# Neighbourhood attention in a hybrid encoder: the raw biases of a pair of heads are asked for ahead of the pair's stack transfers

## The chip, the cores and the metric

The kernel runs on one core of a Trainium2 chip. The metric is the device time of one execution in microseconds (us). The engines are called PE (TensorE), DVE (VectorE), ACT (ScalarE), POOL (GpSimd) and SP (SyncE, which here only issues DMA transfers).

## The reference

Two layers of an encoder, 512 tokens of width 1024, all in float32. Each layer has a half-step feed-forward block, a mixer of three attention branches, and a second half-step feed-forward block. The change touches branch A, the neighbourhood attention: eight heads of 64 channels, tokens laid out as 8 rows of 64 columns, each query attending to all 8 rows and to 16 columns around its own, with a bias per head that depends on the distance in rows and columns.

```python
scores = jnp.einsum('bhrcd,bhrijd->bhrcij', qg, kg).astype(jnp.float32) * (d ** -0.5)
bias = rpb[:, dr[:, None, :, None], dc[None, :, None, :]]
scores = scores + bias[None].astype(jnp.float32)
scores = jnp.where(col_ok[None, None, None, :, None, :], scores, NEG)
p = jax.nn.softmax(scores.reshape(b, h, rows, GRID_W, kr * GRID_W), axis=-1)
out = jnp.einsum('bhrcij,bhrijd->bhrcd', p, vg)
```

## The kernel before

A float32 product is made of three fp32r matmuls (L322, L323, L324), each operand split into a high and a low half. These, called dense matmuls below, fill PE; the attention's own small matmuls are woven between them. The mixer is a list of units in a string, ORDER, that begins "qa0 qa1 aa0 aa1 qa3 qa2 aa3 aa2"; `do(u)` builds one unit after the other. Unit qa*i* makes the projections of head pair *i* (in `qkv_a`), unit aa*i* its attention (`attn_a`, which calls `softmax_pv` once for each of its two heads). Inside the mixer a scheduler sets the order on each engine from the dependences and its own costs, so the order of the text is only one of its inputs.

- `stacks(x, both)` splits a projection into hi (ACT, L348) and lo (DVE, L349) and copies the halves with DMAs on SP's queue into stacked tiles st and sw (L1342, L1343, L1347, L1348). A pair needs four for the queries and eight for the keys, 128 KB each.
- `turn` transposes the values (L1355) and splits them (ACT L1361, DVE L1362).
- `softmax_pv` computes four blocks of scores (L1385, two matmuls each). DVE adds the bias and keeps the extremum nmx (L1388), ACT takes the exponential (L1397), DVE scales by the reciprocal (L1402, L1404), PE transposes (L1412), the halves hi and lo of the transposed block are made (L348, L349) and PE multiplies the values with them (L1415 with hi, L1416 with lo).
- `biases(hd)` loads braw, the raw bias of one head, 256 KB, on SP's queue (L1450), and makes from it and two mask tiles the tiles bedge and bmid with four DVE operations (L1458).

The masks, braw, bedge and bmid all come from one pool with tag "g" of ten buffers, so a late request for a buffer waits until an early user of it is done. The scores' PSUM banks (tag "at") are three, so the third and fourth score block wait for DVE to read an earlier one.

Of the kernel before, what the change touches and what calls it, by code (L numbers as in the profile page):

```python
# [62 lines left out]
RPBW = 64  # L63
# [52 lines left out]
def encoder_kernel(ctx: ExitStack, tc: tile.TileContext, order, xT, wts, cols, rows, rpb, consts, tables, out):  # L116
    nc = tc.nc
# [25 lines left out]
    def nm(s):  # L143
        serial[0] += 1
        return f"{s}{serial[0]}"

    def big(tag, dt=F32, shape=(P, T), name="v"):
        if tag in BUFS:
            return sb.tile(list(shape), dt, tag=tag, name=nm(name), bufs=BUFS[tag])
        kind, pool = phase[0]  # L150
        return pool.tile(list(shape), dt, tag=tag, name=nm(name), bufs=ABUFS[kind][tag])
# [105 lines left out]
    for l in range(L):  # L257
        for which in (1, 2):
            name = f"ffn{which}_w_down"
            places = {(k, u): quarter(k, u) for k in ("11", "12", "21", "22") for u in range(KS // 2)}  # L260
            places.update({(f"n{n + 1}", u): (2 * u, HB * n) for n in range(2) for u in range(KP // 2)})
            for key, (r, c) in places.items():
                src = wts[(NSTREAM + len(extra)) // WB].rearrange("p (a b) -> p a b", a=2)
# [77 lines left out]
    def dense1(name, l, c, X, r0=0, tag="mm", midway=None):  # L341
        return dense([(name, l, r0, c)], X, (tag,), midway=midway)[0]
# [97 lines left out]
    class Handover:  # L440
# [94 lines left out]
        def turn(self, tb):  # L535

            src = self.value if self.following else self.hold
            for n in range(2):
                for k in range(HB):
                    PE.transpose(self.banks[tb][n][:, k * P : (k + 1) * P], src(tb, n)[:, k * P : (k + 1) * P], ident)  # L540
# [893 lines left out]
    def mixer(l, op, first):  # L1434
# [7 lines left out]
        for c0, n in ((0, 512), (512, 256)):  # L1442
            m = big("g", name="mask")
            nc.sync.dma_start(m[:, :n], tables[:, 1024 + c0 : 1024 + c0 + n])
            for b in range(0, n, 256):
                masks[(c0 + b) // 256] = m[:, b : b + 256]

        def biases(hd):
            raw = big("g", name="braw")
            nc.sync.dma_start(raw, bass.AP(rpb.tensor, (l * 8 + hd) * 16 * RPBW, [[RPBW, 8], [1, 16], [1, 8 * RPBW]]))  # L1450
            edge = big("g", name="bedge")
            mid = big("g", shape=(P, 2 * P), name="bmid")

            def put(dst, mask, n0, n1):

                src = raw[:, 7 * RPBW + 39 - 8 * n0 :]
                (ps0, pn), _ = src.ap
                V.tensor_tensor(  # L1458
                    out=dst.rearrange("p (d r c) -> p d r c", r=8, c=8),
                    in0=bass.AP(src.tensor, src.offset, [[ps0, pn], [-8, n1 - n0], [-RPBW, 8], [-1, 8]]),  # L1460
                    in1=mask.rearrange("p (d r c) -> p d r c", r=8, c=8),
                    op=ALU.add,
                )

            put(edge[:, 0:256], masks[0], 0, 4)
            put(mid, masks[1], 0, 4)
            put(edge[:, 256:384], masks[2][:, :P], 2, 4)
            put(edge[:, 384:512], masks[2][:, P:], 0, 2)
            return lambda i: edge[:, 0:256] if i == 0 else edge[:, 256:512] if i == NT - 1 else mid


        def plain(acc, p, scale=1.0):
            x = big("tx", name="x")
            A.activation(natural(x) if p else x, perm(acc) if p else acc, AF.Copy, scale=scale)
            return x
# [12 lines left out]
        def qkv_a(q, k, v):  # L1488
            sq, sk = stacks(plain(q, True, 0.125), False), stacks(rolled(k), True)
            return sq, sk, turn(rolled(v), 2)  # L1490
# [3 lines left out]
        def attn_a(p, sq, sk, vof):  # L1494
            o = big("t", name="o")
            for s in range(2):
                softmax_pv(
                    sq[s], sk[s], lambda j, s=s: vof(j, s), biases(2 * p + s), 1.0, None,
                    perm(o[64 * s : 64 * s + 64, :]), natural, SEEN_A,
                )  # L1500
            OT["a", p] = tuple(t[:, p, :] for t in oa)
            A.activation(OT["a", p][0], o, AF.Copy)
            V.tensor_tensor(out=OT["a", p][1], in0=o, in1=f(OT["a", p][0]), op=ALU.subtract)
# [4 lines left out]
        def attn_b(p, sq, skb, vofb):  # L1508
            o = big("t", name="o")
            for s in range(2):  # L1510
                hd = 2 * p + s
                kv = hd // 4
                softmax_pv(
                    sq[s], skb[kv], lambda j, kv=kv: vofb(j, kv), bias_b, 0.125,
                    (sink[:, l, hd : hd + 1], nsink[:, l, hd : hd + 1]),
                    o[64 * s : 64 * s + 64, :], lambda ap: ap, SEEN_B,
                )
            OT["b", p] = split(o, "g")
# [58 lines left out]
        def gates(n, *ms):  # L1577
            for m in ms:
                pg = dense1(w, l, GL + n * KD + m, X)
                t = gate0[m // 4][:, m % 4, :] if n == 0 else big("g", name="gate")  # L1580
                A.activation(t, pg, AF.Tanh, scale=0.5, bias=col("b_gate", l, n * KD + m))
                gate[n, m] = t

        def combine(n, key, *ms):
            for m in ms:
                py = dense1("w_branch", l, m, [OT[key, k] for k in range(4)], r0=n * 4)
                t = gate.pop((n, m))
                V.scalar_tensor_tensor(out=t, in0=t, scalar=1.0, in1=py, op0=ALU.add, op1=ALU.mult)
                if n == 0:
                    merged[m] = t  # L1590
                else:
                    G.tensor_tensor(out=merged[m], in0=merged[m], in1=t, op=ALU.add)

        def qkv_b(c):
            return stacks(rope(dense1(w, l, c, X), cosR, sinR), c == KB)

        def qkv_c(hd):
            sq = stacks(rope(dense1(w, l, QC + hd, X), cosR, sinR), False)
            sk = stacks(rope(dense1(w, l, KC + hd, X), cosR, sinR), True)
            return sq, sk, turn(plain(dense1(w, l, VC + hd, X), False), 1)  # L1600

        def finish_c(hd):
            A.activation(totc[hd], totc[hd], AF.Sqrt)
            V.reciprocal(out=totc[hd], in_=totc[hd])
            rep = spread(totc[hd], NT)
            V.scalar_tensor_tensor(
                out=oc[hd], in0=oc[hd], scalar=gsub[:, l : l + 1], in1=rep, op0=ALU.mult, op1=ALU.mult
            )
            OT["c", hd] = split(oc[hd], "g")
# [3 lines left out]
        def do(u):  # L1613
            kind, i = u[:2], int(u[2:] or 0)
            if kind == "qa":
                if i == 0:
                    held[u] = qkv_a(*first)
                else:
                    early = second if i == 1 else []
                    late = [dense1(w, l, c + i, X) for c in (QA, KA, VA)[len(early) :]]  # L1620
                    held[u] = qkv_a(*early, *late)
            elif kind == "kb":
                held["kb"] = qkv_b(KB), turn(plain(dense1(w, l, VB, X), False), 2)
            elif kind == "qb":
                held[u] = qkv_b(QB + i)
            elif kind == "qc":
                held[u] = qkv_c(i)
            elif kind == "aa":
                attn_a(i, *held.pop(f"qa{i}"))
            elif kind == "ab":  # L1630
                attn_b(i, held.pop(f"qb{i}"), *held["kb"])
            elif kind == "ac":
                attn_c(*held.pop(f"qc{i}"))
            elif kind == "fc":
                finish_c(i)
            elif kind[0] == "g":
                gates("abc".index(kind[1]), i)
            elif kind[0] == "y":
                combine("abc".index(kind[1]), kind[1], i)

        for u in ORDER.split():
            do(u)
# [75 lines left out]
    for l in range(L):  # L1718
        with open_phase("f"):
            X, accs = ffn(l, 1, X, accs)  # L1720
        with open_phase("m"):
            X, accs = mixer(l, X, accs)
        with open_phase("f"):
            X, accs = ffn(l, 2, X, accs)
# [59 lines left out]
```

## Time and profile before

| what | us |
|---|---|
| median of 3 timed runs (2399.48 to 2400.63) | 2400.39 |
| the profiled execution | 2402.65 |
| its span from the first to the last instruction | 2400.9 |
| PE busy in it | 2373.5 |
| DVE, ACT busy | 1780.8, 1342.4 |

A busy time is a sum over instructions; the end of a matmul is modelled, so an idle time on PE shows where it waited and what a wait cost only nearly. The granted clock is 0.998 of full speed over the span. The part of layer 0 that matters lies from 355 to 430 us, that of layer 1 from 1553 to 1620 us.

### The profile page before, as it was taken

What the parts mean: (1) busy time and instruction counts of PE and PEld (TensorE: products, weight loads), DVE (VectorE), ACT (ScalarE), POOL (GpSimd) and SP (SyncE); (2) the same over time, 40 slices, a digit from 0 to 9 for tenths busy, and PEclk for the clock granted to TensorE, in tenths of its full rate; (3) what the DMA queues carried; (4) which work ended last, traced back from release to release, by engine and by line L of the source; (5) the groups of instructions that cost most, each with busy time, mean ns of one, the idle gap of its engine ahead of it and who ended that gap; (6) DMA issues with size and microseconds to landing.
All of it is one profiled execution on the core that took longest, in us unless ns stands there. A gap on an engine that the chain in (4) does not pass through costs nothing. (4 is left out here: it accounts for less than half of the span.)

```text
span 2400.9 us, 37750 instructions
## 1 busy us (share of the span) xinstructions
PE 2373.5 (99%) x14266; PEld 2080.6 (87%) x14266; DVE 1780.8 (74%) x2960; ACT 1342.4 (56%) x2493; POOL 192.7 (8%) x192
## 2 busy tenths in 40 slices
PE   9999999999999999999999999999999999999998
PEld 8999887888877889998899998878877778899987
DVE  7887975757667467888878878766676764788796
ACT  6565655646555365555655555566555554556563
POOL 0111000000111100110001110000011111011100
PEclk9999999999999999999999999999999999999999
DMA  5566536435443334664525565374354333246642
GB/s 168 161 171 187 165 139 176 128 106 154 109 133 97 100 112 140 160 167 166 171 93 167 159 176 192 118 188 118 111 146 127 107 99 123 97 144 173 186 146 90
DMA packets 119190, 340.46 MB, mean 142 GB/s; under 512 B 15968, under 2 KB 22752, under 8 KB 118496
## 3 DMA queue, kind: packets, MB, share of 16 engines
q1 hardware_dynamic: 91344, 224.72, 30.1%
q10 hardware_dynamic: 22032, 79.78, 11.0%
q0 software_dynamic: 5632, 33.56, 6.9%
q8 instruction: 112, 1.84, 0.3%
q14 instruction: 70, 0.57, 0.1%
HBM read 285.03 MB, written 48.23 MB: 139 GB/s over the span
## 5 line engine op out<-in xcount | busy, mean ns | idle before, releaser
L322 PE MATMUL mm<-X,w 128*128 128x512 f32 (+1 forms) x1044 | 396.5, 380 | 3.9 <-ACT X L618 2.1
L323 PE MATMUL mm<-X,w 128*128 128x512 f32 (+1 forms) x1044 | 396.6, 380 | 0.7 <-DVE X L550 0.7
L324 PE MATMUL mm<-X,w 128*128 128x512 f32 (+1 forms) x1044 | 396.3, 380 | 0.0
L221 DVE TENSOR_TENSOR w<-wr,w 128x512 fp32r<-128x512 f32 x360 | 255.2, 714 | 167.4 <-ACT w L220 166.1
L220 ACT ACTIVATE w<-wr 128x512 fp32r<-128x512 f32 x360 | 223.4, 627 | 224.5 <-PE mm L324 177.6
L878 PE MATMUL mm<-ht,l 128*128 128x256 f32 x1120 | 311.0, 278 | 0.0
L878 PE MATMUL mm<-ht,h 128*128 128x256 f32 x1120 | 310.9, 278 | 0.0
L878 PE MATMUL mm<-lt,h 128*128 128x256 f32 x1120 | 310.5, 277 | 0.0
L322 PEld LDWEIGHTS mm<-X,w 128*128 128x128 f32 x1044 | 197.3, 189 | 35.9 <-ACT X L549 2.6
L323 PEld LDWEIGHTS mm<-X,w 128*128 128x128 f32 x1044 | 197.3, 189 | 32.5 <-DVE X L550 1.1
L324 PEld LDWEIGHTS mm<-X,w 128*128 128x128 f32 x1044 | 197.1, 189 | 30.8
L878 PEld LDWEIGHTS mm<-lt,h 128*128 128x128 f32 x1120 | 210.7, 188 | 0.0
L878 PEld LDWEIGHTS mm<-ht,l 128*128 128x128 f32 x1120 | 210.6, 188 | 0.0
L878 PEld LDWEIGHTS mm<-ht,h 128*128 128x128 f32 x1120 | 210.5, 188 | 0.0
L1119 PE MATMUL mm<-wh,f 128*128 128x512 f32 x640 | 200.2, 391 | 0.0
L878 PE MATMUL mm<-X,h 128*128 128x256 f32 x1120 | 198.8, 277 | 0.0
L878 PEld LDWEIGHTS mm<-X,h 128*128 128x128 f32 x1120 | 169.8, 188 | 0.5 <-DVE v L932 0.2
L878 PE MATMUL mm<-X,l 128*128 128x256 f32 x560 | 154.8, 276 | 0.0
L1119 PEld LDWEIGHTS mm<-wh,f 128*128 128x128 f32 x640 | 120.2, 188 | 25.5
L734 DVE TENSOR_TENSOR l<-wr,h 128x1024 fp32r<-128x1024 f32 x70 | 85.7, 1224 | 66.1 <-PE mm L878 66.1
L1119 PE MATMUL mm<-wl,f 128*128 128x512 f32 x320 | 125.5, 392 | 0.0
L348 ACT ACTIVATE hi<-at 128x256 fp32r<-128x256 f32 (+2 forms) x168 | 73.9, 453 | 73.3 <-PE at L1412 34.7
(372 smaller groups left out, 5425.7 us busy)
## 6 DMA issues: line engine op xcount, KB each, us to landing
wr<-in_wts_dram SPq DMA_DIRECT2D x223, 512.0 KB, 4.7
wr<-in_wts_dram ACTq DMA_DIRECT2D x152, 512.0 KB, 3.6
sum<-in_wts_dram POOLq DMA_DIRECT2D x64, 512.0 KB, 5.5
st<-hi SPq DMA_DIRECT2D x84, 128.0 KB, 2.4
st<-lo SPq DMA_DIRECT2D x84, 128.0 KB, 3.3
ap<-in_wts_dram SPq DMA_DIRECT2D x20, 512.0 KB, 6.8
a<-kept SPq DMA_DIRECT2D x32, 256.0 KB, 6.0
ap<-sum SPq DMA_DIRECT2D x16, 512.0 KB, 3.2
```

Source lines behind the costliest of these rows:

```text
L220: A.activation(hi, raw, AF.Copy)
L221: V.tensor_tensor(out=lo, in0=raw, in1=f(hi), op=ALU.subtract)
L322: PE.matmul(acc, w[0], x[0], start=start, stop=False)
L323: PE.matmul(acc, w[0], x[1], start=False, stop=False)
L324: PE.matmul(acc, w[1], x[0], start=False, stop=stop)
L348: A.activation(hi, src, AF.Copy)
L734: V.tensor_tensor(out=W[g]["l1"], in0=raws[g][0], in1=f(W[g]["h1"]), op=ALU.subtract)
L878: PE.matmul(acc, ws[i], xs[j], start=start and k == n == 0, stop=stop and k == HK - 1 and n == 2, skip_group_check=True,)
L1119: PE.matmul(acc, x[i], w[j], start=start and n == 0, stop=stop and n == 2, skip_group_check=True)
```

## The change: when the raw biases are asked for

A function `fetch_bias(hd)` asks for the raw bias of a head and keeps its tile in a dictionary. `do` calls it for both heads of pair *i* at the start of unit qa*i*, ahead of the projections and stacks of that pair. `biases(hd)` takes the tile from there. The transfers, their sizes, their queue and the arithmetic stay the same. In the changed kernel the lines behind `biases` have numbers that are 8 higher (L1458 becomes L1466, L1482 of ACT becomes L1490), and the request is L1454.

```diff
--- before.py
+++ after.py
@@ -1445,9 +1445,17 @@
             for b in range(0, n, 256):
                 masks[(c0 + b) // 256] = m[:, b : b + 256]
 
+        raws = {}
+
+        def fetch_bias(hd):
+            if hd not in raws:
+                raws[hd] = big("g", name="braw")
+                src = bass.AP(rpb.tensor, (l * 8 + hd) * 16 * RPBW, [[RPBW, 8], [1, 16], [1, 8 * RPBW]])
+                nc.sync.dma_start(raws[hd], src)
+
         def biases(hd):
-            raw = big("g", name="braw")
-            nc.sync.dma_start(raw, bass.AP(rpb.tensor, (l * 8 + hd) * 16 * RPBW, [[RPBW, 8], [1, 16], [1, 8 * RPBW]]))
+            fetch_bias(hd)
+            raw = raws.pop(hd)
             edge = big("g", name="bedge")
             mid = big("g", shape=(P, 2 * P), name="bmid")
 
@@ -1613,6 +1621,8 @@
         def do(u):
             kind, i = u[:2], int(u[2:] or 0)
             if kind == "qa":
+                for s in range(2):
+                    fetch_bias(2 * i + s)
                 if i == 0:
                     held[u] = qkv_a(*first)
                 else:
```

The scheduler reacts to it. In the following pieces a name's number tells one tile of that name from the next; numbers of the two kernels are not the same. The engines are shown in layer 0; layer 1 has the same order.

SP before, from the end of pair 1's stack transfers (sw, st are stacks, hi and lo the halves they are copied from); the first two raws belong to heads 0 and 1:

```order
L1347 DMA sw_4138<-lo_4126 64x512
L1348 DMA sw_4138<-hi_4125 64x512
L1450 DMA braw_4156<-in_rpb_dram 128x1x512
L1450 DMA braw_4232<-in_rpb_dram 128x1x512
L1342 DMA st_4570<-hi_4566 64x512
L1342 DMA st_4573<-hi_4566 64x512
L1343 DMA st_4570<-lo_4567 64x512
L1450 DMA braw_4311<-in_rpb_dram 128x1x512
L1343 DMA st_4573<-lo_4567 64x512
```
SP in the changed kernel, first from the masks on (the raws are those of heads 0 and 1, the stacks those of pair 0):

```order
L1444 DMA mask_3991<-in_tables_dram 128x512
L1444 DMA mask_3993<-in_tables_dram 128x256
L1454 DMA braw_3999<-in_rpb_dram 128x1x512
L1454 DMA braw_4001<-in_rpb_dram 128x1x512
L1342 DMA st_4009<-hi_4005 64x512
L1343 DMA st_4009<-lo_4006 64x512
```
and from the end of pair 0's stacks on (the raws are those of heads 2 and 3, the stacks those of pair 1):

```order
L1343 DMA st_4028<-lo_4019 64x512
L1347 DMA sw_4031<-lo_4019 64x512
L1348 DMA sw_4031<-hi_4018 64x512
L1454 DMA braw_4048<-in_rpb_dram 128x1x512
L1454 DMA braw_4050<-in_rpb_dram 128x1x512
L1342 DMA st_4124<-hi_4120 64x512
```
The raws of heads 0 and 1 have moved ahead of all 24 stack transfers of pairs 0 and 1, those of heads 2 and 3 between the two sets of twelve. The four raws of pairs 3 and 2 stand together behind pair 1's stacks.

DVE before, up to the first reads of scores (braw_4156 is the raw of head 0, w a dense weight's low half, v the values' low half):

```order
L221 TENSOR_TENSOR w_4483<-wr_4466,w_4483 128x512
L1362 TENSOR_TENSOR v_4149<-at_4144,v_4149 128x4x64
L221 TENSOR_TENSOR w_4501<-wr_4499,w_4501 128x512
L1362 TENSOR_TENSOR v_4150<-at_4144,v_4150 128x4x64
L221 TENSOR_TENSOR w_4516<-wr_4499,w_4516 128x512
L1458 TENSOR_TENSOR bedge_4158<-braw_4156,mask_3991 128x256
L1458 TENSOR_TENSOR bmid_4159<-braw_4156,mask_3991 128x256
L1458 TENSOR_TENSOR bedge_4158<-braw_4156,mask_3993 128x128 x2
L1388 ISA s_4165,nmx_4164<-at_4166,bedge_4158 128x256
L1388 ISA nmx_4164 128x1
L1388 ISA s_4165,nmx_4164<-at_4170,bmid_4159 128x256
```
DVE in the changed kernel (braw_3999, braw_4001 and braw_4048 are the raws of heads 0, 1 and 2; lo_4134 is the low half of pair 1's keys):

```order
L1466 TENSOR_TENSOR bmid_4165<-braw_3999,mask_3991 128x256
L1466 TENSOR_TENSOR bedge_4164<-braw_3999,mask_3993 128x128
L349 TENSOR_TENSOR lo_4134<-x_4130,hi_4133 128x512
L1466 TENSOR_TENSOR bedge_4164<-braw_3999,mask_3993 128x128
L1466 TENSOR_TENSOR bedge_4238<-braw_4001,mask_3991 128x256
L1466 TENSOR_TENSOR bmid_4239<-braw_4001,mask_3991 128x256
L1466 TENSOR_TENSOR bedge_4238<-braw_4001,mask_3993 128x128 x2
L1466 TENSOR_TENSOR bedge_4315<-braw_4048,mask_3991 128x256
L1466 TENSOR_TENSOR bmid_4316<-braw_4048,mask_3991 128x256
L1466 TENSOR_TENSOR bedge_4315<-braw_4048,mask_3993 128x128
L1388 ISA s_4171,nmx_4170<-at_4172,bedge_4164 128x256
L1388 ISA nmx_4170 128x1
```
Ahead of the first read of a score stand the bias operations of three heads instead of one, with the low half of pair 1's keys among them. The two v and the w of the piece before have moved behind the first head's scores.

PE before, around the third block of scores of head 0 (at_4174; mm are dense products):

```order
L1385 MATMUL at_4170<-sw_4021,st_4005 128x256
L323 MATMUL mm_4465<-X_3647,w_4080 128x512
L324 MATMUL mm_4465<-X_3646,w_4080 128x512
L322 MATMUL mm_4465<-X_3646,w_4080 128x512
L323 MATMUL mm_4465<-X_3647,w_4080 128x512
```
and, twelve dense matmuls further on:

```order
L324 MATMUL mm_4465<-X_3648,w_4095 128x512
L1385 MATMUL at_4174<-st_4018,st_4005 128x256
L1385 MATMUL at_4174<-sw_4021,st_4005 128x256
L322 MATMUL mm_4465<-X_3648,w_4095 128x512
L323 MATMUL mm_4465<-X_3649,w_4095 128x512
```
PE in the changed kernel, from the second to the fourth block of scores of head 0:

```order
L1385 MATMUL at_4176<-st_4022,st_4009 128x256
L1385 MATMUL at_4176<-sw_4025,st_4009 128x256
L323 MATMUL mm_4469<-X_3647,w_4088 128x512
L324 MATMUL mm_4469<-X_3646,w_4088 128x512
L322 MATMUL mm_4469<-X_3646,w_4088 128x512
L1385 MATMUL at_4180<-st_4022,st_4009 128x256
L1385 MATMUL at_4180<-sw_4025,st_4009 128x256
L323 MATMUL mm_4469<-X_3647,w_4088 128x512
L1385 MATMUL at_4184<-st_4022,st_4009 128x256
L1385 MATMUL at_4184<-sw_4025,st_4009 128x256
```
The third and the fourth block, which stood 17 and 33 dense matmuls behind the second, now stand 3 and 4 behind it. The first transpose of head 0 (L1412) stands 33 dense matmuls earlier than before, the first score blocks of the second, third and fifth head stand 32, 38 and 11 earlier. Ahead of the first scores and behind the attention of branch A, PE's order is that of before.

## Rows read from the trace of the kernel before

**Rows 1.** The page's part 1: busy us (share of the span) and instructions
```profile
PE 2373.5 (99%) x14266; PEld 2080.6 (87%) x14266; DVE 1780.8 (74%) x2960; ACT 1342.4 (56%) x2493; POOL 192.7 (8%) x192
```

**Rows 2.** Timeline of PE: start, us long, instruction [idle before <-releaser]
```profile
394.89 0.39 PE L1385 MATMUL at<-st,st 128*128 128x256 f32 x1 [0.89 <-DVE nmx L1388]
...
395.11 0.28 PE L1385 MATMUL at<-sw,st 128*128 128x256 f32 x1
...
403.15 0.39 PE L1416 MATMUL o<-lo,v 128*128 128x256 f32 x1 [0.81 <-DVE lo L349]
...
416.51 0.39 PE L1416 MATMUL o<-lo,v 128*128 128x256 f32 x1 [0.73 <-DVE lo L349]
...
1582.33 0.38 PE L1385 MATMUL at<-st,st 128*128 128x256 f32 x1 [0.98 <-DVE nmx L1388]
...
1590.44 0.39 PE L1416 MATMUL o<-lo,v 128*128 128x256 f32 x1 [0.64 <-DVE lo L349]
...
1603.70 0.39 PE L1416 MATMUL o<-lo,v 128*128 128x256 f32 x1 [0.65 <-DVE lo L349]
```

**Rows 3.** DVE's waits, 375:480, then 1550:1670: us, times, longest
```profile
DVE bedge L1458 <- DMA braw<-in_rpb_dram: 4.3, 3, 1.9
...
DVE bedge L1458 <- DMA braw<-in_rpb_dram: 5.0, 3, 2.2
```

**Rows 4.** Windows: busy us of each engine, granted clock, DMA share, GB/s
```profile
360.00:370.00 10.00, 10.00 (x75) 9.55 (x74) 4.15 (x6) 4.93 (x9) 0.00 (x0) 1.00 0.42 124
...
380.00:480.00 100.00, 97.47 (x517) 79.72 (x516) 74.18 (x223) 63.33 (x167) 1.29 (x1) 1.00 0.56 151
...
1560.00:1570.00 10.00, 10.00 (x48) 8.26 (x46) 4.43 (x8) 5.26 (x11) 0.00 (x0) 1.00 0.99 239
```

**Rows 5.** Timeline of SP: start, us long, what it issues
```profile
368.05 0.53 SPq L1342 DMA_DIRECT2D st<-hi  x1
...
375.30 0.60 SPq L1348 DMA_DIRECT2D sw<-hi  x1
...
1555.23 0.90 SPq L1444 DMA_DIRECT2D mask<-in_tables_dram  x2
...
1556.24 0.47 SPq L1342 DMA_DIRECT2D st<-hi  x1
...
1564.45 0.62 SPq L1348 DMA_DIRECT2D sw<-hi  x1
```

**Rows 6.** Chain of waits, 1555:1605: start, us to landing
```profile
1563.81 4.25 DMA sw<-lo
...
1574.72 5.96 DMA braw<-in_rpb_dram
...
1584.63 4.44 DMA braw<-in_rpb_dram
```

**Rows 7.** Timeline of PE at the first scores of layer 1
```profile
1573.22 0.28 PE L1385 MATMUL at<-sw,st 128*128 128x256 f32 x1
...
1573.34 0.39 PE L323 MATMUL mm<-X,w 128*128 128x512 f32 x1
...
1573.57 0.39 PE L324 MATMUL mm<-X,w 128*128 128x512 f32 x1
```

**Rows 8.** Timeline of DVE at the first head of layer 0
```profile
393.33 0.43 DVE L1458 TENSOR_TENSOR bedge<-braw,mask 128x256 f32<-128x256 f32 x1 [0.88 <-DMA braw<-in_rpb_dram]
...
394.41 0.42 DVE L1388 CUSTOM_DVE_ANT_0 s<-at,bedge 128x256 f32<-128x256 f32 x1
...
398.54 1.14 DVE L1404 TENSOR_SCALAR s<-s,l 128x256 f32<-128x256 f32 x4
```

**Rows 9.** Timelines of DVE, then ScalarE, in layer 1
```profile
1568.83 0.69 DVE L349 TENSOR_TENSOR lo<-x,hi 128x512 fp32r<-128x512 f32 x1 [0.93 <-ACT hi L348]
...
1571.66 0.55 ACT L1482 ACTIVATE x<-mm 128x448 f32<-128x448 f32 x1 [2.09 <-PE mm L324]
```

**Rows 10.** Timeline of PE: first score of the fifth head, layer 0
```profile
424.27 0.36 PE L1385 MATMUL at<-st,st 128*128 128x256 f32 x1
```

## The prediction, made blind

> **What bounds the kernel now.** I read the page's busy times first: TensorE (PE) is busy 2373.5 of 2400.9 us [rows 1], so almost nothing can be won off PE, and the question is which of its 27 us of idle time the late biases own. The profiled execution took 2402.65 us, the three timed runs have their median at 2400.39; the sum is made in differences on the trace and put against 2400.39.
>
> Next, PE's timeline in the two stretches of neighbourhood attention (from 385 us in layer 0, from 1572 us in layer 1). Six instructions there stand behind idle time [rows 2]: in each layer one score matmul that waits for VectorE (DVE) to read an earlier score, and two value matmuls (L1416) that wait for DVE's lo half. DVE's waits say why [rows 3]: three times per layer the bias operation waits for braw, 4.3 and 5.0 us in all, and in DVE's order a score or a lo half stands right behind it. From 380 to 480 us PE is busy 97.47 of 100 us [rows 4]; the three idles of layer 0 are 2.43 of the missing 2.53. Nothing else is to be had there.
>
> **Part 1, what can go.** Idle before the six: 0.89 + 0.81 + 0.73 = 2.43 us in layer 0 and 0.98 + 0.64 + 0.65 = 2.27 in layer 1. A stall costs more than its idle time, as a matmul of 512 columns is shown 0.39 us long and yet is followed after 0.23 [rows 7]: 0.16 us of the matmul ahead would have been overlapped, and the restarted one of 256 columns lets the next follow after 0.22 us (394.89 to 395.11 in rows 2) where 0.12 is usual (1573.22 to 1573.34 in rows 7), 0.1 more. So 6 x 0.26 = 1.56 on top of 4.70: at most 3.2 us in layer 0 and 3.05 in layer 1, 6.25 in all (0.26% of the time). The operation counts are those of before, and the matmuls outside the attention stand in the same order; so the sum is this gain less what new waits cost.
>
> **Part 2, layer 0.** SP sends the masks and then has to wait for the first stack, which goes out at 368.05 [rows 5]; the DMA engines are busy 0.42 of the time from 360 to 370 us [rows 4]. The two raws of pair 0 fall into this gap and cost nothing. Those of pair 1 go out behind pair 0's twelve stack transfers, the last of which leaves at 375.30 [rows 5], so from 376 us. With 4.44 to 5.96 us to land [rows 6] they are there at 380.4 to 382, and the first scores come at 385.5: cover of 3 us. All three stalls go.
>
> What is late next: PE now reaches the first transpose of the probabilities (L1412) 33 dense matmuls, 7.6 us, earlier. From the start of the first score it has ahead of it eight score matmuls (0.12 each, 1.0 us with the restart) and 3 + 16 dense ones of 0.23, 5.4 us. The softmax needs, in the rows of before [rows 8], from the first score's start on DVE at 394.41 to the end of the first of four scales (398.54 + a quarter of 1.14 = 398.83) 4.4 us (ScalarE's exponentials lie in it); with half a microsecond, an estimate, from PE's score to DVE's (two matmuls of 0.28 behind one another, rows 7) that is 4.9: half a microsecond of cover. The lo halves of the first head now also share DVE and ScalarE with the halves of pair 1's values, which used to be done before. Below, this costs nothing; above, eight heads at the tenth of a microsecond and one full stall like those of rows 2 would be 1.0 + 0.3. I take **0.4 us** a layer, near the lower end, since the later heads of before are woven as closely and show no idle at all. Layer 0: -3.2 + 0.4 = **-2.8**.
>
> **Part 3, layer 1.** Here the same edit meets another stretch. The masks go out only at 1555.23, and the stacks of pair 0 follow at 1556.24 without a gap [rows 5]. From 1560 to 1570 us the DMA engines are at 0.99 with 239 GB/s [rows 4]: nothing is hidden. Two raws of 256 KB are 524 KB; at 239 GB/s that is 2.2 us, more than the 1.2 that SP spends on issuing two transfers (0.62 for the one at 1564.45, rows 5). Everything behind them in SP's queue moves by some 2.2 us. Ends of this term: 1.2 (issue alone) and 2.2; I take 2.2, since the share is 0.99.
>
> Then: the last stack of pair 0 is issued at 1566.7 instead of 1564.45 [rows 5] and the raws of pair 1 at 1567.3. Landing 4.44 to 5.96 us later [rows 6], they are there at 1571.7 to 1573.3. Three bias operations of that raw stand ahead of DVE's first score (1.08 us for four, from 393.33 to 394.41 in rows 8, so 0.9 for three): the score starts at 1572.6 to 1574.2, and its nmx is there 0.42 later [rows 8], 1573.0 to 1574.6. PE's third score, which waits for that, would stand at 1573.34 [rows 7] + 3 x 0.23 = 1574.0. So the stall is 0 to 0.6, and with the restart 0.9. The lo half of pair 1's keys, ahead of all this on DVE, moves too: it starts at 1568.83 today, behind a ScalarE hi of about the same 0.69 us [rows 9], which fits the stack that was issued at 1563.81 and landed 4.25 later, at 1568.06 [rows 6], and freed its buffer. With 2.2 on top that is 1570.3, hi and lo are done at 1571.6, and the copy for L1355 queued behind them on ScalarE, which starts at 1571.66 today [rows 9], keeps its time with nothing to spare. Upper end: if the raws of pair 1 also pay the queue that grew by 2.2 us, they take 8.2 us, and the stall is 2.8 + 0.26 = 3.1. Lower end 0. I take **1.2**, closer to the 5.96 that a first raw took in this layer. Ties as in layer 0: 0.4. Layer 1: -3.05 + 1.2 + 0.4 = **-1.45**.
>
> On that term the Trainium skill has two rules. On its page "DMA: Bandwidth & Descriptors", section "Queues, rings and completion order", each engine takes descriptors in ring order, so raws ahead of stacks delay the stacks; it speaks against this change, and without it the delay would be 1.2 instead of 2.2 us and the time about 2395.1; the full DMA share from 1560 us goes with the rule, no run so far shows it. In the same page's "Anatomy of one DMA — SWDGE (gpsimd) path" a transfer costs about 2.0 us + bytes / 436e3; an estimate by it is 2.6 us for a raw, with which layer 1 would have no stall and the sum 2394.9; the rows' 4.44 to 5.96 us differ, and the measurement decides.
>
> **Later raws.** Those of pairs 3 and 2 are asked for together and wait on SP for bias buffers that the scores of heads 0 and 1 free, at about 398 us in layer 0 by the times above (the first head's scores from 386, the second's 11 us on); behind them stand the stacks of the next two pairs. The new hold leaves pair 3's twelve transfers, at some 0.6 us each [rows 5] 8 us, to be issued by 406 to 408 and landed by 413, while their first scores come at 424.27 today [rows 10] and, 11 dense matmuls and the stalls earlier, at about 419: free with 6 us of cover, and pair 2's stand behind them.
>
> Sum: -2.8 - 1.45 = -4.25, so 2400.39 - 4.25 = **2396.1 us**. By the ends it is 2394.1 (no new stall) to 2400.4 - 6.25 + 3.1 + 2.6 = 2399.9.
>
> **Rivals.** (a) All six stalls go and none comes: 2400.39 - 6.25 = 2394.1. For it: one raw landed in 4.44 us, and PE's other heads run without idle. It holds if the raws of pair 1 land by 1572.7 in layer 1. Against: the share of 0.99.
> (b) Layer 1 gives back what layer 0 gains: the transfers simply land late in a full queue, PE waits about 3 us for the stacks at L1355 or L1385 and 3 for the raws, where it waited 3.05: -2.8 + 3 = 2400.6, no change. It decides from a delay of the stacks of 5 us instead of 2.2.
> (c) Slower: the closer weave doesn't hold. Before, 33 more matmuls stood between a first score and its transposes; now each head's lo half comes just in time. If the two halves of values and probabilities come late in every one of the 16 heads by a stall as in rows 2 (0.65 to 0.89, say 0.75, + 0.26 = 1.0), that is +16 - 6.25 = 2410. It passes the bound of +0.2% from 0.7 us a head on. Against it: at least ten of the sixteen heads of before show no idle in their weave (six stalls in all).
> (d) The change does nothing, as the scheduler could leave the bias operations where they were: excluded by the new order on DVE and PE, but for a small rest; 2400.4.
>
> **How the numbers follow.** A difference under 0.2%, 4.8 us, is about what a measurement of this kernel can't tell from none: faster is below 2395.6, slower above 2405.2. My case (2395.0 to 2398.6) has 0.53, (a) 0.20, (b) 0.16, (c) 0.08, (d) 0.03. Faster: (a) and the lowest part of mine, 0.34. Slower: (c), 0.08. Same: the rest, 0.58. The range goes from (a) to (b), 2394.0 to 2400.6; (c) and the tails are left out.
>
> **What would show it.** In the profile after: DVE waits for braw gone in layer 0 and under 2 us in layer 1; the value matmuls' two idles gone per layer; PE from 380 to 480 us busy over 99.3 of 100; SP's raws at about 358 and 376 us, and 1556 and 1567. Wrong if PE's idle at L1412, L1415 or L1416 is over 1 us in a layer (the weave), if the third score's idle in layer 1 is 0 or over 3, or if idle shows up at the next pairs' first scores (SP's hold).

## The result, and the profile after

| | before | after |
|---|---|---|
| median, 16 runs each (us) | 2400.89 | 2405.16 |
| lowest to highest | 2399.48 to 2403.58 | 2401.80 to 2407.13 |
| the profiled execution's span | 2400.9 | 2404.1 |
| granted clock over the span | 0.998 | 0.998 |

The ratio is 1.0016, with an interval of 1.0009 to 1.0023: slower by about 4 us, a difference below the bound of 0.2%, and above the forecast range, which ended at 2400.6.

To see where the time went, I took the starts of the same dense matmul in both traces (PE issues the same 12,648 of them in both kernels, those of the feed-forward blocks at L878 and L1119 counted in): number 2400, just ahead of the first scores of layer 0, to number 2680 behind that attention, and 8755 to 9035 in layer 1. The first stretch took 93.81 us before and takes 94.21 now, the second 93.27 and 97.12: +0.40 and +3.85. The rest of the program, which no edit touches, comes to -1 us in this pair of traces (span +3.2). Both stretches start 0.80 us later in the changed kernel's trace than in that of before, so times of the two traces are that far apart at the same place of the program. The two attentions didn't gain 2.8 and 1.45; they lost.

PE's waits of the changed kernel, first 375 to 480 us, then 1550 to 1670 (us in all, times, longest):

```profile
PE at L1385 <- DVE nmx L1388: 2.0, 1, 2.0
...
PE at L1355 <- ACT x L1491: 4.9, 1, 4.9
```

All six idles of [rows 2] are gone, and each layer has one new one. The timeline of PE (start, us long, instruction, [idle before <- releaser]) around both:

```profile
389.69 0.38 PE L1385 MATMUL at<-st,st 128*128 128x256 f32 x1 [2.02 <-DVE nmx L1388]
...
390.05 0.63 PE L323 MATMUL mm<-X,w 128*128 128x512 f32 x1
...
391.33 0.63 PE L322 MATMUL mm<-X,w 128*128 128x512 f32 x1
391.76 0.63 PE L323 MATMUL mm<-X,w 128*128 128x512 f32 x1
...
393.44 0.39 PE L324 MATMUL mm<-X,w 128*128 128x512 f32 x1
...
1578.20 1.11 PE L1355 MATMUL at<-cons,x 128*128 128x128 f32 x4 [4.88 <-ACT x L1491]
```

Two things stand in these lines. PE waited longer in one piece than in any of the stalls that were removed. And behind the wait the dense matmuls follow each other after 0.43 us (391.33 to 391.76), where 0.23 is usual [rows 7], for some three microseconds. The windows say why (us, PE busy (x), granted clock, DMA share, GB/s of PE's rows):

```profile
389.00:394.00 5.00, 4.32 (x14) 0.66 0.77 199
394.00:396.00 2.00, 2.00 (x12) 1.00 0.92 221
1578.00:1583.00 5.00, 4.80 (x21) 0.68 0.78 204
```

After the wait PE runs at its lower level, 1.2 of 2.4 GHz, and comes back to 1.00 (from 1583 us on in layer 1). From 390.05 to 393.44 us stand seven dense and two score matmuls, which at the usual distances (0.23 and 0.12) take 1.85 us and took 3.39: 1.54 lost to the clock. From 1578.20 to 1581.24 stand four transposes, four score and three dense matmuls, 0.41 (as from 385.84 to 386.25 in the same timeline) + 0.55 + 0.69 = 1.65 at full clock, and they took 3.04: 1.39 lost. With the 0.26 us of a restart as in Part 1 the new stalls cost 2.02 + 0.26 + 1.54 = 3.82 and 4.88 + 0.26 + 1.39 = 6.53. Taken from the stretches' +0.40 and +3.85, what the six old stalls gave back is 3.42 and 2.68, 6.1 together, where Part 1 had 6.25.

**Where the stall of layer 0 comes from.** DVE waits for braw once from 375 to 480 us, where [rows 3] had three waits and 4.3 us (in layer 1 it is one of 0.4 for three of 5.0 together):

```profile
DVE bedge L1466 <- DMA braw<-in_rpb_dram: 2.8, 1, 2.8
```

DVE's timeline in layer 0 shows where that wait stands now. The bias of head 2 is ahead of the first read of a score of head 0, and that read is what PE's third score block needs:

```profile
388.32 0.43 DVE L1466 TENSOR_TENSOR bedge<-braw,mask 128x256 f32<-128x256 f32 x1 [2.77 <-DMA braw<-in_rpb_dram]
...
389.20 0.42 DVE L1388 CUSTOM_DVE_ANT_0 s<-at,bedge 128x256 f32<-128x256 f32 x1
```

That raw was forecast for 380.4 to 382 and was there at 388.3. SP's timeline, as in [rows 5], has both causes, layer 0 first:

```profile
358.61 1.46 SPq L1454 DMA_DIRECT2D braw<-in_rpb_dram  x2
...
375.67 0.59 SPq L1343 DMA_DIRECT2D st<-lo  x1
379.73 0.46 SPq L1347 DMA_DIRECT2D sw<-lo  x1
...
380.88 1.34 SPq L1454 DMA_DIRECT2D braw<-in_rpb_dram  x2
...
1557.25 1.39 SPq L1454 DMA_DIRECT2D braw<-in_rpb_dram  x2
...
1566.79 0.46 SPq L1347 DMA_DIRECT2D sw<-lo  x1
...
1571.67 0.60 SPq L1348 DMA_DIRECT2D sw<-hi  x1
1572.31 1.35 SPq L1454 DMA_DIRECT2D braw<-in_rpb_dram  x2
```

SP stands still from 376.26 to 379.73, and its waits name the reason (365 to 400 us, then 1550 to 1600):

```profile
SPq L1347 <- DMA wr<-in_wts_dram: 3.4, 1, 3.4
...
SPq L1347 <- DMA braw<-in_rpb_dram: 3.1, 2, 2.0
SPq L1347 <- DMA wr<-in_wts_dram: 2.0, 1, 2.0
```

A stack transfer doesn't use a weight tile (wr) or a raw. What it waits for is the program's count of transfers under way: SP's and ACT's transfers take eight semaphores in turn, so that a new one waits until the eighth before it has landed, whatever that carried and whichever engine issued it. The trace's records bear this out: the weight fetch of 375.14 and the stack transfer of 379.73 carry the same semaphore, and so do the weight fetch of 1562.47 and the stack transfer of 1571.16. ACT had asked for 512 KB of weights at 375.14, and SP's stack could not leave before they were there. The kernel before has such a wait in the same stretch, and I had not read it:

```profile
SPq L1342 <- DMA wr<-in_wts_dram: 3.5, 1, 3.5
```

There it held pair 1's first stack transfer, for which nobody was in a hurry. In the changed kernel the two raws of pair 0 take two turns of the eight ahead of the stacks, so the turn of the same weight fetch comes two transfers earlier, at pair 0's eleventh; behind it the raws of pair 1 are held too. The remaining delay is the landing itself, 380.88 to 388.3, 7.4 us, where [rows 6] had 4.44 to 5.96.

**Where the stall of layer 1 comes from.** The raws of pair 0 left as forecast (1557.25), but stack transfers behind them had to wait until they were there, sw up to 1566.79, 9.5 us after the first of them had left. The last stack left at 1571.67, not at 1566.7. The chain of waits has the rest (start, us, what):

```profile
1562.47 8.68 DMA wr<-in_wts_dram
1571.16 0.46 SPq L1347
...
1572.94 3.67 issue
1576.71 0.70 DVE lo L349
1577.49 0.54 ACT x L1490
1578.20 1.11 PE at L1355 x4
```

The weight fetch held SP to 1571.16; ScalarE's next hi starts at 1575.97, 4.3 us after the last stack was issued (the profile names no releaser there; it fits the 4.25 of [rows 6], after which the buffer of pair 1's keys is free); DVE's lo and ScalarE's copy x follow, and PE's transposes of the values wait for x. It is the chain that Part 3 described around [rows 9]: the copy x starts 5.8 us later than there (1577.49 for 1571.66), 0.8 of it the distance of the two traces.

The second window of [rows 4] as it is now, 380 to 480 us:

```profile
380.00:480.00 100.00, 97.98 (x515) 80.54 (x514) 75.94 (x224) 64.23 (x170) 1.29 (x1) 0.98 0.56 146
```

PE is not busier than before by the 1.8 us that Part 2 and the last part of the prediction wanted, and its mean clock is 0.98. From 1560 to 1570 us the DMA engines are less full than before, 0.88 for 0.99 with 205 for 239 GB/s; SP stood still for a part of that time.

### The profile page after: what moved, and what is told of

Read it like the earlier page. It is cut to its first block, busy times and chain, and to the rows that moved or that the text cites. A ratio compares the mean times of both kernels' runs of the same rounds, so it can differ in the third digit from the quotient of the medians.

```text
span 2404.1 us, 37763 instructions
## 1 busy us (share of the span) xinstructions
PE 2373.7 (99%) x14266; PEld 2080.8 (87%) x14266; DVE 1782.2 (74%) x2960; ACT 1341.7 (56%) x2493; POOL 192.5 (8%) x192
## 5 line engine op out<-in xcount | busy, mean ns | idle before, releaser
L878 PE MATMUL mm<-ht,l 128*128 128x256 f32 x1120 | 311.0, 278 | 0.0
L878 PE MATMUL mm<-ht,h 128*128 128x256 f32 x1120 | 310.9, 278 | 0.0
L878 PE MATMUL mm<-lt,h 128*128 128x256 f32 x1120 | 310.6, 277 | 0.0
L878 PEld LDWEIGHTS mm<-lt,h 128*128 128x128 f32 x1120 | 210.8, 188 | 0.0
L878 PEld LDWEIGHTS mm<-ht,l 128*128 128x128 f32 x1120 | 210.6, 188 | 0.0
L878 PEld LDWEIGHTS mm<-ht,h 128*128 128x128 f32 x1120 | 210.6, 188 | 0.0
L1119 PE MATMUL mm<-wh,f 128*128 128x512 f32 x640 | 200.2, 391 | 0.0
L878 PE MATMUL mm<-X,h 128*128 128x256 f32 x1120 | 198.9, 277 | 0.0
L878 PEld LDWEIGHTS mm<-X,h 128*128 128x128 f32 x1120 | 170.1, 188 | 0.3
L878 PE MATMUL mm<-X,l 128*128 128x256 f32 x560 | 154.9, 277 | 0.0
L1119 PEld LDWEIGHTS mm<-wh,f 128*128 128x128 f32 x640 | 120.2, 188 | 25.5
L1119 PE MATMUL mm<-wl,f 128*128 128x512 f32 x320 | 125.5, 392 | 0.0
```

Source lines behind the costliest of these rows:

```text
L878: PE.matmul(acc, ws[i], xs[j], start=start and k == n == 0, stop=stop and k == HK - 1 and n == 2, skip_group_check=True,)
L1119: PE.matmul(acc, x[i], w[j], start=start and n == 0, stop=stop and n == 2, skip_group_check=True)
```

## Experiments

Two theories stood against each other. **A**: SP is held until transfers have landed that it doesn't need, ScalarE's weight fetch above all; that makes the stacks and the second pair of raws late. **B**: the raws' bytes are too many for a stretch in which the DMA engines are busy anyway; they land late themselves and push the stacks behind them. In the table the two stretches are those from above, in us against before (93.81 and 93.27), each from the one profiled execution.

| kernel | median us | ratio to before | layer 0 stretch | layer 1 stretch |
|---|---|---|---|---|
| changed kernel | 2405.16 | 1.0016 [1.0009, 1.0023] | +0.40 | +3.85 |
| e1, raws behind the stacks | 2415.08 | 1.0061 [1.0049, 1.0074] | +6.18 | +7.60 |
| e2, pair 0 ahead, others behind | 2411.74 | 1.0052 [1.0039, 1.0065] | +2.88 | +8.76 |
| e3, weights on POOL's queue | 2399.72 | 0.9997 [0.9988, 1.0006] | -2.94 | +3.24 |
| e4, raws on POOL's queue | 2394.21 | 0.9978 [0.9969, 0.9987] | -2.52 | -2.35 |
| e5, as e4, but held back | 2410.50 | 1.0042 [1.0028, 1.0056] | +3.14 | +7.45 |
| e6, raws first on SP | 2407.47 | 1.0025 [1.0015, 1.0034] | -0.80 | +8.02 |
| e7, small raws | 2398.09 | 0.9987 [0.9978, 0.9996] | -3.02 | -0.64 |
| e8, small raws, weights on POOL | 2395.48 | 0.9976 [0.9967, 0.9986] | -3.31 | -2.78 |

The medians of before beside them were 2400.37 (e1 to e4), 2401.57 (e5 to e7) and 2400.03 (e8). e1, e2 and e5 have 5 runs, the others 10 or 11. All edits are against the changed kernel, and `...` stands for lines left out.

### e1: the raws of a pair behind its own stacks

```diff
             if kind == "qa":
-                for s in range(2):
-                    fetch_bias(2 * i + s)
                 if i == 0:
...
                     held[u] = qkv_a(*early, *late)
+                for s in range(2):
+                    fetch_bias(2 * i + s)
```

> The raws of each pair are asked for right behind the stacks of that pair instead of ahead of them. Theory A (the queue is held: raws ahead of the stacks, and the completion waits that come with the new order, delay stacks and the raws of pair 1): stacks go out as in the kernel before, SP's 3.4 us wait for a weight fetch between pair 0's stacks is gone, all six old stalls are gone and no new one comes: PE idle under 0.5 us in either attention stretch, no stretch at the lower clock, 6 us under the kernel before (2394.9). Theory B (512 KB more in a crowded stretch, wherever they stand): the same here. Theory C (the closer weave on PE and DVE is what stalls): part of the gain is lost in each of the heads, 2398 or more.

It was the slowest of all, +0.61%. SP's timeline, DVE's and PE's in layer 0:

```profile
378.65 1.44 SPq L1454 DMA_DIRECT2D braw<-in_rpb_dram  x2
...
393.69 2.36 SPq L1454 DMA_DIRECT2D braw<-in_rpb_dram  x2
...
399.14 0.43 DVE L1466 TENSOR_TENSOR bedge<-braw,mask 128x256 f32<-128x256 f32 x1 [4.14 <-DMA braw<-in_rpb_dram]
...
403.45 1.54 PE L1412 MATMUL at<-cons,s 128*128 128x128 f32 x6 [5.47 <-DVE s L1404]
```

The stacks of pair 0 are out at 375.2, as nothing is ahead of them, but the raws behind them wait 3.4 us for the same weight fetch (the last one is out at 374.64 + 0.59, the raws leave at 378.65), and those of pair 1 leave at 393.69 only. The scheduler still puts the bias of pair 1 on DVE ahead of the reciprocal of head 0, presumably as it takes the raws to be there by then; so DVE stands still on a transfer that no one needs yet, and PE's transposes of head 0 wait 5.47 us (5.16 in layer 1). My expectation had looked at SP's queue and not at what stands behind the bias on DVE. The kernel doesn't tell A from B; it shows that asking behind the stacks doesn't move the bias of pair 1 back far enough on DVE.

### e2: only pair 0's raws ahead

```diff
-                for s in range(2):
-                    fetch_bias(2 * i + s)
+                for s in range(2 if i == 0 else 0):
+                    fetch_bias(s)
...
                     held[u] = qkv_a(*early, *late)
+                    for s in range(2):
+                        fetch_bias(2 * i + s)
```

> The raws of pair 0 stay ahead of pair 0's stacks, those of the other pairs move behind their own stacks. Theory A: layer 0 loses its new stall (2.0 us idle and the lower clock after it), since no raw of pair 1 stands ahead of DVE's first score any more, and keeps the gain of 3.1; layer 1 keeps stacks behind raws, so PE still waits 4 to 5 us at L1355 and has the lower clock for some 4 us: +4 there, in all about +1 against the kernel before (2401.9). Theory B gives the same in layer 1. Theory C: no stall in either layer, -6 (2394.9).

PE's timeline, both layers:

```profile
401.51 1.26 PE L1412 MATMUL at<-cons,s 128*128 128x128 f32 x6 [2.76 <-DVE s L1404]
...
1580.68 1.12 PE L1355 MATMUL at<-cons,x 128*128 128x128 f32 x4 [5.75 <-ACT x L1491]
```

Layer 0 fails in the manner of e1: the second raw of pair 1 leaves at 392.52 only, late for DVE's order. Layer 1 has the wait of the changed kernel, at the same line and 0.9 us longer, and one of 2.11 us at L1416. There one of pair 1's raws still leaves right behind pair 0's last stack (1574.15), the other 14 us later (1588.14). Both are issued behind all stacks of pair 0, so the stall at L1355 hangs on pair 0's raws, which stand ahead of the stacks, or on the hold. A and B are both left.

### e3: the weights of unit qa3 on POOL's queue (the holds for weights taken away)

```diff
         for u in ORDER.split():
+            stream["eng"] = G if u == "qa3" else nc.scalar
             do(u)
```

> The change as it is, but the weight fetches made while unit qa3 is built go out on POOL's queue instead of ScalarE's; SP's and DVE's order stay as in the changed kernel, and no stack has to wait for the completion of a weight fetch. Theory A: the 3.4 us hold in layer 0 goes, the raws of pair 1 leave at about 376.5 and land by 383, the stall at the third score goes (under 0.5 us); in layer 1 the hold of 2.0 to 2.5 us goes and the 4.9 us at L1355 fall to about 2.5; in all 3 to 5 us under the changed kernel (2400 to 2402). Theory B (bytes): both stalls stay within 0.5 us of 2.0 and 4.9, time within 1 us of the changed kernel.

By the ratios 0.19% under the changed kernel; no difference from before can be told. In layer 0 the hold is gone. SP's timeline there, with PE's at its one stall of layer 1, and then SP's longest wait for raws from 1550 to 1585 us (us, times, longest):

```profile
377.16 1.33 SPq L1454 DMA_DIRECT2D braw<-in_rpb_dram  x2
...
1572.82 1.11 PE L1355 MATMUL at<-cons,x 128*128 128x128 f32 x4 [3.03 <-ACT x L1491]
```

```profile
SPq L1348 <- DMA braw<-in_rpb_dram: 5.3, 2, 4.1
```

The two raws of pair 1 leave 3.7 us earlier than in the changed kernel. The first takes as long to land as there, 7.1 us for 7.4 (by the trace's records of its semaphore it is there at 384.3), yet PE doesn't wait at all from 375 to 480 us: the stretch is 2.94 shorter, as Part 2 had forecast (2.8). So in layer 0 the stall goes with the hold for weights alone. In layer 1 PE's wait at L1355 falls from 4.88 to 3.03 but stays; SP is still held there until raws have landed, a part of A that this edit doesn't take away.

### e4: the raws on POOL's queue

```diff
-                nc.sync.dma_start(raws[hd], src)
+                G.dma_start(raws[hd], src)
```

> The change as it is, but the raws go out on POOL's queue instead of SP's: same bytes, as early or earlier, not in SP's queue and not among its completion waits. Theory A: stacks leave SP as in the kernel before, no stall at L1355 or at the third score, 5 to 6 us under the kernel before (2395 to 2396). Theory B: in layer 1 the raws still compete with pair 0's stacks from 1556 us on, the stacks land 2 us or more later and PE waits 2 us or more at L1355 or L1385.

6.2 us under before by the medians, a ratio of 0.9978: the fastest kernel with the whole computation. POOL's timeline in layer 1:

```profile
1542.53 2.44 POOL L1454 DMA_DIRECT2D braw<-in_rpb_dram  x4 [134.39 <-PE o L540]
```

The windows (us, busy of PE, PEld, DVE, ACT, POOL, granted clock, DMA share, GB/s); in layer 0, from 375 to 475 us, PE is busy 99.73:

```profile
1535.00:1550.00 15.00, 15.00 (x129) 15.00 (x128) 7.56 (x14) 6.26 (x13) 2.44 (x4) 1.00 0.45 121
1565.00:1665.00 100.00, 100.00 (x530) 82.58 (x529) 72.39 (x209) 64.36 (x169) 3.65 (x5) 1.00 0.54 142
```

POOL has nothing ahead of the raws, so all four leave from 15 us before the first of the changed kernel (11 us, if both are counted from dense matmul 8755), while the DMA engines are at 0.45. Two things have changed here, the queue and the time; e5 separates them.

### e5: POOL's queue at the changed kernel's time

To e4's edit a gate is added: the raws of pair 0 are held until cosR has landed, those of pair 1 until the last stack of pair 0 has.

```diff
+                if i < 2:
+                    gate = cosR if i == 0 else f(held["qa0"][1][1][1])
+                    paced([lambda s=s: fetch_bias(2 * i + s) for s in range(2)], gate[:, :1])
...
```

> The raws go out on POOL's queue, but not early: those of pair 0 wait until cosR has landed (about 1559 us in layer 1, when the changed kernel asks for them), those of pair 1 until the last key stack of pair 0 has landed. So the same bytes run beside the same stacks, but not ahead of them in SP's queue and not among SP's completion waits. Theory A (held queue): the stacks leave SP as in the kernel before, no idle over 1 us at L1355 in layer 1, none over 0.7 at the third score, time 2395 to 2398. Theory B (bytes): pair 0's stacks land 2.2 us later or more, PE waits 1.5 to 3 us at L1355 in layer 1 and has the lower clock after it, 2400 or more.

Everything that e4 had won is gone, and more. POOL, DVE and PE in layer 0, then PE in layer 1:

```profile
379.73 1.29 POOL L1454 DMA_DIRECT2D braw<-in_rpb_dram  x2 [0.46 <-issue]
...
388.93 0.42 DVE L1466 TENSOR_TENSOR bedge<-braw,mask 128x256 f32<-128x256 f32 x1 [5.65 <-DMA braw<-in_rpb_dram]
...
390.29 0.58 PE L1385 MATMUL at<-st,st 128*128 128x256 f32 x1 [4.67 <-DVE nmx L1388]
...
1576.93 0.66 PE L1355 MATMUL at<-cons,x 128*128 128x128 f32 x4 [2.77 <-ACT x L1491]
1582.69 0.58 PE L1385 MATMUL at<-st,st 128*128 128x256 f32 x1 [3.57 <-DVE nmx L1388]
```

The view of the tile braw has the time from issue to landing of the two raws of 379.73:

```profile
DMA to landing us min/median/max: 8.6/8.7/8.8
```

They take 8.6 to 8.8 us in a queue of their own, with the DMA engines at 1.01 from 379.7 to 389 us. The two raws that the same kernel sends in the same queue at 358.38 land in 4.0 and 4.9 us. So it isn't SP's queue that makes raws slow, but what the DMA engines carry at that time: B. And in layer 1 the values are late at L1355 by 2.77 us without a raw in SP's queue ahead of the stacks. The gates open a little later than the changed kernel asks: counted from dense matmuls 2400 and 8755, pair 1's raws leave 0.7 us later in layer 0 and 2.6 in layer 1, so the waits at L1385 are in part the gate's.

### e6: four raws first in SP's queue

```diff
...
+        for hd in range(4):
+            fetch_bias(hd)
         masks = {}
         for dst, c0 in ((cosR, 0), (sinR, 512)):
```

> The raws of pairs 0 and 1 are asked for on SP's queue ahead of cosR and the masks, at the very start of the mixer; SP reaches them before it waits for PE, some 14 us earlier in layer 1. Theory A and B alike (what counts is that no raw stands between or beside the stacks): no new stall, all six old ones gone, 5 to 6.5 us under the kernel before (2394 to 2395.5). If it is the engine that asks (POOL instead of SP) that made the run with POOL's queue fast, the stalls stay: 2399 or more.

The function `fetch_bias` moves up too. This was to be e4 without POOL, and it failed. SP's wait at the raws of layer 1 (us, times, longest), and the timelines of SP, DVE and PE there:

```profile
SPq L1445 <- PE mm L324: 15.6, 1, 15.6
```

```profile
1552.74 2.80 SPq L1445 DMA_DIRECT2D braw<-in_rpb_dram  x4
...
1569.81 0.42 DVE L1468 TENSOR_TENSOR bedge<-braw,mask 128x256 f32<-128x256 f32 x1 [10.27 <-DMA mask<-in_tables_dram]
...
1579.19 1.12 PE L1355 MATMUL at<-cons,x 128*128 128x128 f32 x4 [3.48 <-ACT x L1493]
```

First in the queue isn't early: SP waited 15.6 us at the first raw for a dense product, and the raws left at 1552.74. That is 15.5 us ahead of dense matmul 8755, where the changed kernel's first raw leaves 13.9 and e4's 25.2 us ahead of it. Now 1 MB stands ahead of masks and stacks; the masks land late, DVE waits 10.27 us for them, a dense weight behind them on DVE is late, and PE has two stalls, 2.74 us at 1572.71 and 3.48 at L1355 (in layer 0 one of 1.19, also at L1355). I did not find out why SP's wait ends so much later than POOL's.

### e7: small raws (the bytes taken away)

Only the first eighth of a raw's columns is loaded (32 KB), POOL sets the rest to zero: seven eighths of the raw bias are left out. The order on SP is not quite kept: pair 0's raws now leave behind that pair's first stack transfer.

```diff
-                nc.sync.dma_start(raws[hd], src)
+                G.memset(raws[hd], 0.0)
+                nc.sync.dma_start(raws[hd][:, :RPBW], bass.AP(rpb.tensor, (l * 8 + hd) * 16 * RPBW, [[RPBW, 8], [1, 16], [1, RPBW]]))
```

> The change as it is, but a raw's transfer brings only an eighth of its columns (32 KB instead of 256 KB) and the rest is zero, set by POOL; so the bias is wrong, and the bytes are gone while the raws keep their place in SP's queue. Theory B (bytes): no stall in either layer, 6 us under the kernel before. Theory A: the waits for the raws' completion get short, but the last stack of pair 0 still waits for a weight fetch: a hold of 2 to 3.5 us on SP in both layers, in layer 1 PE waits 1 to 2.5 us at L1355; in layer 0 the raw of pair 1 still lands in time, as it takes 3 us instead of 7; in all 1 to 4 us under the kernel before.

By the ratios 0.29% under the changed kernel. SP's wait from 365 to 400 us, and PE's timeline in layer 1:

```profile
SPq L1348 <- DMA wr<-in_wts_dram: 2.0, 1, 2.0
```

```profile
1571.57 0.65 PE L1355 MATMUL at<-cons,x 128*128 128x128 f32 x4 [0.96 <-ACT x L1491]
```

In layer 0 a hold for weights of 2.0 us (for 3.4) is left and PE has no wait. So there, as in e3, taking one of the two away is enough: the stall came of both together. In layer 1 the hold is still there with 2.1 us and still costs 0.96 us at L1355 (and 0.79 at the third score); the rest of the 4.88 went with the bytes.

### e8: small raws, and the weights on POOL's queue (both taken away)

The edits of e7 and e3 together.

> Both cuts together: a raw's transfer brings an eighth of its columns (the bias is wrong, 224 KB of each raw are left out), and the weight fetches of unit qa3 go out on POOL's queue, so that no stack waits for the completion of one. Theory A+B (in layer 1 the stall of the changed kernel is made of the raws' bytes and of SP's hold for a weight fetch, and of nothing else): no hold over 0.7 us between pair 0's key stacks, idle at L1355 and the third score under 0.5 us together, layer 1 2 to 3.5 us under the kernel before, layer 0 about 3 under it, 2394 to 2396 in all. If a third cause is there (the raws' two places in SP's queue as such, or the order on DVE), a stall of 1 us or more stays in layer 1, as with small raws alone (0.96 + 0.79).

PE's windows, columns as for e4:

```profile
375.00:475.00 100.00, 100.00 (x532) 82.85 (x531) 75.59 (x222) 65.08 (x171) 3.81 (x6) 1.00 0.54 140
1565.00:1665.00 100.00, 100.00 (x532) 82.97 (x531) 74.42 (x217) 64.43 (x169) 3.35 (x6) 1.00 0.52 135
```

PE has no idle time in either attention. The two stretches are 3.31 and 2.78 us shorter than before, 6.1 together: what Part 1 said the six stalls were worth (6.25), with no new stall against it. The hold and the bytes together are the whole cause: in e8 too raws stand ahead of and between the stacks on SP, and the bias of pair 1 stands on DVE ahead of the first read of a score (383.28 and 385.95 us in layer 0), and no stall comes of it. In PE's idle time their shares in layer 1 nearly add up: of the 4.88 us, 1.85 go without the hold for weights (3.03 stay) and 3.13 without the bytes (0.96 + 0.79 stay). In the stretch they don't, as the 3.03 us of e3 still bring the lower clock (0.50 in the 4.2 us behind it): it is 0.6 us shorter without the hold, 4.5 without the bytes and 6.6 without both. A late raw is itself one of the landings for which SP is held.

## Why the prediction was wrong

- **Part 1, what can go: right.** 6.25 was forecast as the most, e8 shows 6.1.
- **Part 2, the closer weave: right, and too dear.** No idle stands at L1412, L1415 or L1416 from 375 to 480 us or from 1550 to 1670. The 0.4 us a layer for ties were not needed; rival (c) is out.
- **Part 2, "those of pair 1 go out ... from 376 us", "cover of 3 us": the step that failed in layer 0.** They left at 380.88 and took 7.4 us. I had read when SP was free of instructions, not what it would wait for: the same wait for wr stood in SP's waits of before, on another transfer. With both terms the raw was at 388.3, 6 us behind my window, and the cover of 3 became a stall of 2.02. By these rows it had to be there by 388.32 - 2.02 = 386.3. With the slow landing alone it was in time (e3: 377.2 + 7.1 = 384.3), with the late issue alone it would have been just about (380.9 + 4.44 to 5.96 = 385.3 to 386.8); e7, with a late issue and few bytes, has no stall there.
- **Part 3, "moves by some 2.2 us": the mis-sized term of layer 1.** The last stack left 7.2 us later than in [rows 5] (6.4 without the distance of the two traces), not 2.2: the bytes' time on the engines was priced, but not that later stacks wait for the raws' landing and, through it, run into ScalarE's weight fetch. The lo half that kept its time "with nothing to spare" was late by the whole excess, and the stall came at L1355 with 4.88 us instead of 1.2 at the third score, where none is left, one of the signs of being wrong that the prediction named. Rival (b) had this place and half of the mechanism (a full queue, without SP's hold), and its condition, a delay of over 5 us, was met. Its layer 1 (+3, as two waits of 3 us) is near the +3.85 that came; its 2400.6 was too low mainly because it kept the gain of 2.8 in layer 0.
- **Not in the sum at all: the clock.** I priced a stall at its idle time and 0.26 us. Behind the two new ones PE ran at 1.2 GHz for some 3 us, 1.54 and 1.39 us more, 2.9 of the 10.4 us that they cost. The Trainium skill ("TensorE: Matmul & The Clock Gate", section "Why this matters for your kernels") says that idle gaps between bursts take PE back to half rate. The wait of 4.88 us, with 0.68 behind it, agrees; the one of 2.02, with 0.66 behind it, is shorter than the gaps that the section warns of, and there the measurement decides.
- **Later raws: right.** SP is held at L1454 for bias buffers (7.4 us in layer 1, by DVE's nmx), and no idle on PE follows from it.
- **The two rules weighed in Part 3.** The Trainium skill ("DMA: Bandwidth & Descriptors", "Queues, rings and completion order") has the descriptors taken in ring order, so that the stacks are late behind the raws. That spoke against the change, and e7 goes with it: with an eighth of the bytes ahead of them the wait at L1355 is 0.96 instead of 4.88 us. But in e5 no raw is in the stacks' queue and the wait is still 2.77, so no run here shows the ring order by itself. By the formula in that page's "Anatomy of one DMA — SWDGE (gpsimd) path" a raw takes an estimated 2.6 us; on POOL's queue 4.0 to 8.9 us were measured (e5), on SP's 7.4 in the changed kernel. The formula has no term for other transfers.

In the terms of the sum: layer 0 was to be -2.8 and was +0.40, layer 1 -1.45 and +3.85. The difference stayed within 0.2%, but not as the small gain that was forecast: it is a gain of 6 and a loss of 10.

## What to carry to other kernels

A transfer that is asked for earlier isn't free because its queue looks idle: see where the DMA engines have room (e4's raws leave at a share of 0.45, and it beats both kernels), and what the issuing engine will wait for there, including landings that have nothing to do with the transfer. Where transfers share a rotation of semaphores, a transfer put in ahead also moves the place at which the later ones wait. A scheduler that believes data to be early puts their user early on an in-order engine; if they are late, everything behind it is. One long wait on PE was dearer here than several short ones: the six of before, of 0.64 to 0.98 us, left the clock alone, and the one of 4.88 cost 1.39 us more than its idle time and restart.

## What the runs showed of the hardware that I had not expected

The granted clock behind a wait of PE, by its idle time, in windows of 3 to 5 us behind it, in the kernels above (waits under 0.5 us left out):

| idle of PE, us | granted clock behind it | kernel |
|---|---|---|
| 0.89, 0.98 | 1.00, 1.00 | before |
| 0.96, 0.79 | 1.00, 1.00 | e7 |
| 1.19 | 1.00 | e6 |
| 1.60 | 1.00 | e1 |
| 2.02, 4.88 | 0.66, 0.68 | changed |
| 0.89, 2.11 | 1.00, 1.00 | e2 |
| 2.74, 3.48 | 0.52, 0.50 | e6 |
| 2.76 | 0.57 | e2 |
| 2.77, 3.57, 4.67 | 0.61, 0.50, 0.59 | e5 |
| 3.03 | 0.50 | e3 |
| 5.16, 5.47 | 0.57, 0.50 | e1 |
| 5.75 | 0.50 | e2 |

In these rows the clock stayed up behind every wait of up to 1.60 us and fell behind every one of 2.74 or more; of the two of 2.02 and 2.11 it fell behind one. What else decides there was not tried. Also not tried was e1 with DVE's order held fast, which would show what raws behind the stacks are worth by themselves.

And a raw of 256 KB, always a transfer of the same form, took from 4.0 us (e5, issued at 358.38) to 8.9 us (e5, at 1560.06) to land in one kernel and one queue; the DMA engines were at 0.59 from 358 to 364 us and at 1.06 from 1560 to 1569 us.
